# Down projection of a gated block as seven products of halves, with bias, compression and merge reordered

## The chip, the cores and the metric

The kernel runs on one core of one Trainium2 chip, as one launch. The metric is device time in microseconds (us), the median over runs. Engines are named as the profile names them: PE (TensorE matmul), DVE (VectorE), ACT (ScalarE), POOL (GpSimd), SP (SyncE, which here only issues DMAs). All tensors are fp32; every large product is made of three passes over tensors that were split into a high and a low part.

## What is computed

One layer of a hybrid decoder trunk over S=1024 tokens with D=1024 columns and F=2816 hidden columns:

```python
h = rmsnorm(x, norm_mix_g)
u, q, kc, vc, ks, vs, kw, vw, g_nsa, g_br = split(h @ w_in)
y_a = s5_mixer(u, ...) @ w_up_ssm            # state space, GELU, GLU
kc, vc = compress(kc, ...), compress(vc, ...) # gelu(blocks @ w1) @ w2
y_b = nsa_mixer(q, kc, vc, ks, vs, kw, vw, gates, rel_bias) @ w_up_nsa
x = x + (sigmoid(g_a) * y_a + sigmoid(g_b) * y_b) @ w_out
h = rmsnorm(x, norm_ffn_g)
x = x + (silu(h @ w_ffn_gate) * (h @ w_ffn_up)) @ w_ffn_down
out = rmsnorm(x, norm_final_g)
```

`rel_bias` is a table of 32 buckets by 8 heads; the attention adds its rows to the scores.

## The kernel before

**Splitting.** Each fp32 operand becomes a high part (ACT or POOL casts it to fp32r) and a low part (DVE subtracts the high part from the operand), in `Kernel.split` (lines 410 to 418). Each product is then three matmuls: high by high, high by low, low by high. Weights come in by DMA into tiles `wr` and are split into `wh` and `wl`. `Weights.next` (helper class at line 70) keeps two weight tiles split and four loaded ahead. The hidden values of the feed-forward come as `sr`, split into `shi` and `slo`.

**Order.** The order of every engine is the order in which the program issues its instructions. SP issues nearly all DMAs, and so takes them one after the other in that order; a DMA that waits holds back those behind it. The stages, in order of time, are these.

- Head: first norm, then `h @ w_in` as 448 groups of three matmuls of 512 columns (lines 406 to 408). The function `along(side, rate)` gives these groups out as cover: each `yield` of a side stage lets `rate` groups pass. The side stages are `s5_params` (line 666), `s5` (line 838), `compress` (line 971) and `glu` (line 1057). `s5_params` holds the bias step at lines 707 to 717: for each of 8 heads one plain fp32 matmul of 384 columns that spreads the bucket table over distances, a copy out of the matmul's bank, and a store to memory. `compress` loads eight weight blocks `w1` into three buffers. `glu` splits the values z of one token half, makes its products, and then does the other half.
- Up projection a (`up_a`), cut into parts of which 12 run ahead of the attention and the others in its first units; attention in 64 units; up projection b.
- Merge (line 1450): `@ w_out` for token tiles in the order of `units(...)`, the addition to x, the second norm (`norm`, `root`, `turned`), and the sums of input quarters that the next stage needs. `turn` runs these sums (T1 to T4, B22). `Winograd.first` (line 260) makes the first unit of the next stage with the last norms in between.
- Gate and up: class `Winograd` (line 123). The 44 blocks of 128 columns of both matrices go as 22 units. A unit forms two blocks (256 columns) for all tokens by seven products of half tokens, half depth and half of the two blocks in place of eight. It is 84 matmuls of 512 columns. POOL, DVE and ACT form sums of weight quarters and of products, and the finished hidden block is stored as two halves of 512 tokens each, `sd[f][0]` and `sd[f][1]`.
- Down (`down`, line 1598): two token halves, 22 blocks f of 128 hidden columns, four token tiles, two column halves, three passes: 1056 matmuls of 512 columns. Each f of a token half is 24 matmuls, one `sr` (256 KB) and one `wr` (512 KB). The first half's results are added to x and normed beside the second half; the second half's are added, normed, scaled and stored behind the last matmul, on DVE, ACT and for two scalings on POOL.

Of the kernel before, what the change touches and what calls it, by code (L numbers as in the profile page):

```python
# [16 lines left out]
P = 128  # L17
# [18 lines left out]
NPOW = 9  # L36

# [85 lines left out]
class Winograd:  # L123
# [136 lines left out]
    def first(self, norms, turn):  # L260
# [6 lines left out]
        self.product(1, 1, x1)  # L267
        next(norms)
        self.t2(0)
# [54 lines left out]
    def rest(self, n, early):  # L324
# [20 lines left out]
        self.t1(n + 1)  # L345
        if last:
            next(self.after)
# [7 lines left out]
        self.out(n, 1, 1, p5)  # L355
        self.product(n, 3, z, first=False)
# [9 lines left out]
        self.out(n, 1, 0, u3)  # L366

    def run(self, after):

        self.after = after  # L370
        for n in range(1, len(self.mats)):
            self.t3(n)
            self.sums(n + 1)
            if n > 1:
                self.p1(n)
            self.rest(n, n == 1)


class Kernel:
# [212 lines left out]
    def in_proj(self, specs, ev):  # L592

        nc = self.nc
        for c0, kind, dst in specs:
            w = self.W.next("w_in", 0, KD, c0, P)
            for h in range(2):
# [5 lines left out]
                elif kind in "qk":  # L603
# [5 lines left out]
                    nc.sync.dma_start(dst[0][:, tok], a.bitcast(F32))  # L609
                    nc.sync.dma_start(dst[1][:, tok], b.bitcast(F32))  # L610
                else:
# [5 lines left out]
                    nc.sync.dma_start(dst[:, tok], a)  # L617
# [20 lines left out]
    def s5_loads(self):  # L638
# [22 lines left out]
        self.rb = x("rb", 32, 8)  # L661
        dma(self.rb, A["rel_bias"])
        self.oh = x("oh", 32, 384)
        dma(self.oh, A["consts"][0:32, 874:1258])

    def s5_params(self):
# [39 lines left out]

        rbb = x("rbb", 32, 8, P)
        V.tensor_copy(rbb, self.rb[:, :, None].to_broadcast([32, 8, P]))
        yield
        for h in range(8):  # L710
            b = self.bank("c")
            nc.tensor.matmul(b[:, 0:384], rbb[:, h, :], self.oh, start=True, stop=True)
            s = tmp.tile([P, 384], F32, name="brs", tag="brs", bufs=2)
            (AC.copy if h % 2 else V.tensor_copy)(s, b[:, 0:384])
            nc.sync.dma_start(self.bd[h], s)
            yield
# [79 lines left out]
        yield  # L796

# [9 lines left out]
        V.tensor_tensor(self.Bq, self.Bq, w, op=OP.subtract)  # L807

# [29 lines left out]
    def s5(self):  # L838
# [63 lines left out]
        yield  # L902
        zb = None
# [67 lines left out]
    def compress(self, pool):  # L971
# [20 lines left out]
        def w1(j):  # L992
            w = pool.tile([P, 4, 256], F32, name="w1", tag="w1", bufs=3)
# [4 lines left out]
        ws = [w1(j) for j in range(3)]  # L998
# [18 lines left out]
        for which in range(2):  # L1017
            t = self.bank("c")
            for j in range(4):
# [6 lines left out]
                if 4 * which + j < 5:  # L1026
                    ws.append(w1(4 * which + j + 3))
# [29 lines left out]
    def glu(self, pool):  # L1057
        nc, V = self.nc, self.nc.vector
        for h in range(2):
            t = slice(512 * h, 512 * h + 512)  # L1060
            z = self.z[h]
            zs = [pool.tile([P, 4, 512], FR, name=n, tag=n) for n in ("zh", "zl")]
            for k in range(4):
                self.split(zs[0][:, k, :], zs[1][:, k, :], z[:, k, :], "act", "dve")
                yield
            yield
            yield
# [126 lines left out]
    def attention(self, pools, loads, up):  # L1194
# [163 lines left out]
        def start(n):  # L1358
            if n == 2:
# [16 lines left out]
            if n == 1:  # L1376
# [73 lines left out]
    def merge(self, pool, m, td, xd, ffn):  # L1450
# [90 lines left out]
        def units(tts, q, between):  # L1541

            banks = [self.bank("a") for _ in tts]
            for u in range(4):
# [13 lines left out]
                for f, *a in between.get(u, ()):  # L1558
                    f(*a)

        T = lambda tt, *what: [(turn, w, tt) for w in what]
        units((0, 1, 4, 5), 0, {(0, "m"): [(load, tt) for tt in (0, 1, 4, 5)] + [(ffn.factors,)],
# [3 lines left out]
                          1: [(turned, 0)] + T(4, "transpose", "sums"), 2: T(4, "T1", "B22")})  # L1566
# [11 lines left out]
    def down_loads(self, pool, sd):  # L1578
# [298 lines left out]
```

## Time and profile before

| | |
|---|---|
| runs | 1617.88, 1622.04, 1624.08 us (median 1622.04) |
| profiled execution | 1624.46 us, span 1622.7 us |
| PE busy | 1561.6 us (96% of the span) |
| DVE busy | 926.8 us (57%) |
| ACT busy | 634.6 us (39%) |
| POOL busy | 637.6 us (39%) |
| mean granted clock of PE | 0.979 |

The span is the time from the first to the last instruction of the profiled execution. A wait in the view of waits is idle time of one engine and the instruction that ended it: "PE c L1023 <- DMA w<-in_cmp_w_k" is a matmul of line 1023 into bank c that waited for a DMA which fills the tile w. A window row gives the busy time of each engine in a stretch, the number of its instructions in parentheses, the granted clock (PEclk), and what the DMA engines did. The end of a matmul is modelled, so the pace of matmuls is read from their starts.

### The profile page before, as it was taken

The numbers are of one execution on the slowest core, as the hardware profiler recorded it, in microseconds if no ns is written. First come the engines' busy times: TensorE is split into PE (matmuls) and PEld (weight loads), VectorE is DVE, ScalarE is ACT, GpSimd is POOL, SyncE is SP. The second block draws the span as 40 slices with busy tenths as digits, with TensorE's granted clock in tenths as the row PEclk, the third lists the DMA queues.
The fourth block names the chain that finished last, engine by engine and source line by source line (L and its number), as shares of the span: only waits on it lengthen the run. The fifth ranks groups of instructions, "written<-read, shape, count | busy, mean of one in ns | idle before, by whom it ended". The sixth has DMA issues, their size and how long they took to land. (4 is left out here: it accounts for less than half of the span.)

```text
span 1622.7 us, 22419 instructions
## 1 busy us (share of the span) xinstructions
PE 1561.6 (96%) x7928; PEld 1310.4 (81%) x7928; DVE 926.8 (57%) x1744; ACT 634.6 (39%) x1277; POOL 637.6 (39%) x740
## 2 busy tenths in 40 slices
PE   8998999998999999999999899999999999999995
PEld 8876888886877899998787777888888888888884
DVE  7346886632245899998857564444444445335433
ACT  5212334421220698898116543332333333233322
POOL 1005777610021455555450038677776661000001
PEclk9999999999999999999999989999999999999998
DMA  6342443339337712100666512223222214454551
GB/s 220 107 146 86 123 130 96 94 87 252 98 112 240 203 30 68 42 27 16 217 197 199 176 46 80 89 79 95 81 79 90 79 52 171 150 205 150 177 198 53
DMA packets 165607, 196.38 MB, mean 121 GB/s; under 512 B 20730, under 2 KB 119446, under 8 KB 165495
## 3 DMA queue, kind: packets, MB, share of 16 engines
q1 hardware_dynamic: 165495, 194.94, 38.7%
q8 instruction: 63, 1.03, 0.3%
q14 instruction: 49, 0.40, 0.1%
HBM read 144.96 MB, written 47.84 MB: 119 GB/s over the span
## 5 line engine op out<-in xcount | busy, mean ns | idle before, releaser
L418 DVE TENSOR_TENSOR wl<-wr,wh 128x1024 fp32r<-128x1024 f32 (+1 forms) x170 | 196.8, 1168 | 144.8 <-ACT wh L415 109.6
L406 PE MATMUL a<-hhi,wh 128*128 128x512 f32 x448 | 182.9, 408 | 0.0
L408 PE MATMUL a<-hhi,wl 128*128 128x512 f32 x448 | 178.0, 397 | 0.0
L407 PE MATMUL a<-hlo,wh 128*128 128x512 f32 x448 | 177.8, 397 | 0.0
L415 ACT CAST wh<-wr 128x1024 fp32r<-128x1024 f32 (+1 forms) x138 | 114.4, 844 | 157.2 <-PE a L220 41.6
L1285 POOL TENSOR_SCALAR P<-P,sum,gates 128x640 f32<-128x640 f32 (+3 forms) x192 | 124.8, 663 | 116.6 <-DVE sum L1279 73.5
L219 PE MATMUL a<-mhi,wh 128*128 128x512 f32 (+1 forms) x360 | 139.1, 386 | 2.2 <-ACT wh L415 1.8
L221 PE MATMUL a<-mhi,wl 128*128 128x512 f32 (+1 forms) x360 | 138.7, 385 | 0.8 <-DVE wl L418 0.8
L220 PE MATMUL a<-mlo,wh 128*128 128x512 f32 (+1 forms) x360 | 138.6, 385 | 0.0
L413 POOL TENSOR_SCALAR wh<-wr 128x1024 fp32r<-128x1024 f32 x32 | 34.0, 1064 | 226.8 <-PE a L407 168.8
L160 POOL TENSOR_SCALAR wr<-wr,gcol 128x256 f32<-128x256 f32 x176 | 92.7, 546 | 72.2 <-DVE mlo L474 67.9
L1314 DVE TENSOR_TENSOR PTl<-T,PTh 128x512 fp32r<-128x512 f32 (+3 forms) x200 | 104.2, 544 | 9.7 <-ACT PTh L1313 7.8
L406 PEld LDWEIGHTS a<-hhi,wh 128*128 128x128 f32 x448 | 85.0, 190 | 24.1 <-issue 6.2
L1265 ACT ACTIVATE P<-P,m 128x640 f32<-128x640 f32 (+7 forms) x128 | 95.7, 747 | 17.5 <-DVE m L1249 17.5
L408 PEld LDWEIGHTS a<-hhi,wl 128*128 128x128 f32 x448 | 85.0, 190 | 20.1
L418 DVE TENSOR_TENSOR slo<-sr,shi 128x512 fp32r<-128x512 f32 x44 | 32.0, 728 | 120.0 <-ACT shi L415 120.0
L407 PEld LDWEIGHTS a<-hlo,wh 128*128 128x128 f32 x448 | 85.1, 190 | 17.7
L1313 ACT CAST PTh<-T 128x512 fp32r<-128x512 f32 (+3 forms) x200 | 88.4, 475 | 20.7 <-PE T L1312 19.3
L1249 DVE CUSTOM_DVE_ANT_0 P<-S,B 128x640 f32<-128x640 f32 (+7 forms) x128 | 89.5, 700 | 5.0 <-PE S L1214 2.1
L418 DVE TENSOR_TENSOR wl<-S,wh 128x1024 fp32r<-128x1024 f32 x44 | 65.5, 1489 | 44.4 <-ACT wh L415 41.2
L1312 PE MATMUL T<-cst,P 128*128 128x128 f32 x592 | 87.2, 274 | 3.4 <-DVE PTl L1314 2.8
L415 ACT CAST shi<-sr 128x512 fp32r<-128x512 f32 x44 | 27.1, 619 | 154.4 <-PE c L1638 153.9
(427 smaller groups left out, 3992.1 us busy)
## 6 DMA issues: line engine op xcount, KB each, us to landing
wr<-in_w_ffn_down SPq DMA_DIRECT2D x44, 512.0 KB, 3.4
wr<-in_w_in SPq DMA_DIRECT2D x28, 512.0 KB, 4.1
wr<-in_w_out SPq DMA_DIRECT2D x24, 512.0 KB, 4.3
wr<-in_w_ffn_gate SPq DMA_DIRECT2D x22, 512.0 KB, 3.9
wr<-in_w_ffn_up SPq DMA_DIRECT2D x22, 512.0 KB, 3.7
sr<-sd SPq DMA_DIRECT2D x44, 256.0 KB, 4.0
gd<-evf SPq DMA_DIRECT2D x32, 256.0 KB, 2.6
Q<-qd SPq DMA_DIRECT2D x64, 128.0 KB, 3.0
```

The source lines that it names most:

```text
L160: self.K.nc.gpsimd.tensor_scalar(t[:, k], t[:, k], self.g[:, 4 * kh + k:4 * kh + k + 1], 1.0, op0=OP.mult, op1=OP.mult)
L219: mm(o, wh[:, k], bh[:, k, c], start=first and k == 0, stop=False, skip_group_check=True)
L220: mm(o, wh[:, k], bl[:, k, c], start=False, stop=False, skip_group_check=True)
L221: mm(o, wl[:, k], bh[:, k, c], start=False, stop=k == 3, skip_group_check=True)
L406: mm(ps, a, c, start=start and k == 0, stop=False, skip_group_check=True)
L407: mm(ps, a, d, start=False, stop=False, skip_group_check=True)
L408: mm(ps, b, c, start=False, stop=stop and k == nk - 1, skip_group_check=True)
L415: nc.scalar.copy(hi, src)
L418: (nc.gpsimd if lo_eng == "pool" else nc.vector).tensor_tensor(lo, src, hi, op=OP.subtract)
L1265: AC.activation(p[:, 0:nk], p[:, 0:nk], AF.Exp, bias=m[:, 0:1], scale=-1.0, accum_out=sm(0))
L1285: sc = lambda x, y, z: GP.tensor_scalar(x, x, a[:, y:y + 1], gate(z), op0=OP.mult, op1=OP.mult)
L1314: V.tensor_tensor(ol, t[:, 0:len(cc), :], oh, op=OP.subtract)
```

## The change

The text of the change has six parts.

1. `down` is one class of products as in gate and up: seven products over half of the tokens, half of the hidden depth (11 blocks) and half of the columns, in the order 1, 5, 6, 3, 7, 2, 4. That is 7 x 11 x 4 x 3 = 924 matmuls of 512 columns in place of 1056. Operands of the products are hidden halves `sd` themselves, or sums of them `ss`, and weight quarters or differences of them, which DVE makes (`combine`) in tiles `b0` to `b2` and `near` that stay loaded. Results are added to x on DVE as each product ends (`beside`).
2. The sums `ss` are made by `chain(f)`: four loads of 256 KB into one tile `ch` (one buffer), four additions and subtractions of 128x512 on DVE, four stores. Nine of the eleven chains run beside the last nine units of gate and up (`next(self.chain, None)` at four places of a unit), the last two beside the first eight blocks of product 1.
3. The end: token tiles 4 to 7 have their right column half done after product 2, so behind the last matmul each tile has one column half to add, square and norm. The last three blocks of product 4 are made tile by tile. POOL has no part in it. The norm and scaling of token tiles 0 to 3 stand beside blocks 3 to 7 of product 4.
4. Bias: the 8 heads go from `s5_params` to the start of `s5` (`bias`), with high and low parts of the table (two fp32r matmuls of 384 columns per head in place of one fp32 matmul). Stores of this step and of the input projection's results go out from ACT's queue.
5. Compression and GLU: four buffers for `w1`, four blocks loaded ahead, and in the first half one more `yield` per block; the second half of z is split before the first half's products.
6. Attention and merge: 10 in place of 12 parts of `up_a` before the attention, three more in its first units. In the merge, the table for the square root is loaded ahead (`one`), `turned(0)` and the sums of tile 5 stand later, and in `first` the sums `t2(0)` and tile 7's transposes and sums stand earlier.

```diff
@@ Winograd.first
+        self.t2(0)
         next(norms)
-        self.t2(0)
...
+        turn("transpose", 7, "ac")
         self.product(0, 2, x0, first=False)
-        turn("transpose", 7, "ac")
+        turn("sums", 7)
         turn("T1", 6)
         self.t3(0)
-        turn("sums", 7)
         self.product(1, 2, x1, first=False)
+        turn("T1", 7)
         self.p2out(0)
-        turn("T1", 7)
@@ Winograd.run
+            f = n - 2
+            self.chain = chain(f) if f >= NF // 2 else iter(())
+            next(self.chain, None)
             self.t3(n)
@@ input projection
-                    nc.sync.dma_start(dst[0][:, tok], a.bitcast(F32))
+                    nc.scalar.dma_start(dst[0][:, tok], a.bitcast(F32))
...
-                    nc.sync.dma_start(dst[:, tok], a)
+                    nc.scalar.dma_start(dst[:, tok], a)
@@ bias
-        for h in range(8):
-            b = self.bank("c")
-            nc.tensor.matmul(b[:, 0:384], rbb[:, h, :], self.oh, start=True, stop=True)
...
+            for i in range(2):
+                nc.tensor.matmul(b[:, 0:384], self.rbb[i][:, h, :], self.ohr, start=i == 0, stop=i == 1)
+            s = pool.tile([P, 384], F32, name="brs", tag="brs", bufs=2)
+            nc.scalar.copy(s, b[:, 0:384])
+            nc.scalar.dma_start(self.bd[h], s)
+            yield
@@ compress
-        ws = [w1(j) for j in range(3)]
+        ws = [w1(j) for j in range(4)]
...
-                if 4 * which + j < 5:
-                    ws.append(w1(4 * which + j + 3))
+                if which == 0:
+                    ws.append(w1(j + 4))
+                    yield
@@ merge
+        one = pool.tile([P, 1], F32, name="one")
+        V.memset(one, 1.0)
+        AC.activation(one, one, AF.Sqrt)
...
-                          1: [(turned, 0)] + T(4, "transpose", "sums"), 2: T(4, "T1", "B22")})
+                          2: [(turned, 0)] + T(4, "transpose", "sums"), (3, "m"): T(4, "T1", "B22")})
...
-                                (2, "m"): [(load, 6), (load, 7)] + T(5, "T1", "B22"), 2: T(5, "T3", "T2"),
-                                (3, "m"): T(5, "T4")})
-        units((2, 3), 1, {})
+                                (2, "m"): [(load, 6), (load, 7)] + T(5, "T1", "B22"), 2: T(5, "T3")})
+        units((2, 3), 1, {0: T(5, "T2"), 1: T(5, "T4")})
@@ chain and down
+    def chain(self, pool, sd, ss, f):
+        nc, V = self.nc, self.nc.vector
+        t, g = pool.tile([P, 4, 512], F32, name="ch", tag="ch", bufs=1), f - NF // 2
+        for i, src in enumerate((sd[g][0], sd[g][1], sd[f][0], sd[f][1])):
+            nc.sync.dma_start(t[:, i], src)
+        yield
+        a, b, c, d = (t[:, i] for i in range(4))
+        V.tensor_tensor(d, b, d, op=OP.add)
+        V.tensor_tensor(b, a, b, op=OP.subtract)
+        yield
+        V.tensor_tensor(a, d, a, op=OP.subtract)
+        V.tensor_tensor(c, c, a, op=OP.subtract)
+        yield
+        for i, n in enumerate((2, 3, 4, 1)):
+            nc.sync.dma_start(ss[g][n], t[:, i])
+        yield
...
+        order = [(p, f) for p in (1, 5, 6, 3, 7, 2, 4) for f in range(NH)]
...
+                if p in (5, 6, 7, 4):
+                    V.tensor_tensor(o, {5: s1, 6: s2, 7: s2, 4: s2}[p], o, op=OP.subtract)
...
+            mm(o, ah[:, t], bh, start=first, stop=False, skip_group_check=True)
+            mm(o, ah[:, t], bl, start=False, stop=False, skip_group_check=True)
+            mm(o, al[:, t], bh, start=False, stop=end, skip_group_check=True)
...
+            if p == 4 and f < 4:
+                V.tensor_tensor(half(4 + f, 1), half(4 + f, 1), gf[:, 512:D], op=OP.mult)
+            if p == 1 and f < 8:
+                if f % 4 == 0:
+                    sums["chain"] = self.chain(pool, sd, ss, NF - 2 + f // 4)
+                next(sums["chain"])
...
+            tt = f - 4
+            if 0 <= tt < 4 and p == 4:
+                scaled(tt, slice(0, D), self.rstd(dn, sums[tt]), "dve")
...
+        for n, (p, f) in enumerate(order[:last]):
+            split(n + 2)
+            load(n + 4)
+            combine(n + 3)
...
+            for tt in range(4):
+                products(n, tt)
+            beside(p, f)
+        split(len(order))
+        for tt in range(4):
+            for n in range(last, len(order)):
+                products(n, tt)
...
+            add(4 + tt, 0, U[tt])
+            square(half(4 + tt, 0), sums[4 + tt][:, 0:1])
+            if tt:
+                finish(tt - 1)
+        finish(3)
```

How the change moves instructions is shown at three places. First, SP's queue where down starts: `sd` is a store of hidden values (the last block's second store is the one from `u`), `sr` and `wr` are loads for down. Before:

```order
L244 DMA sd_8684<-p_12603 128x512
L244 DMA sd_8685<-u_12686 128x512
L1586 DMA sr<-sd_8651 128x512
L83 DMA wr<-in_w_ffn_down 128x1024
L1586 DMA sr<-sd_8653 128x512
```

And now, with the stores of the ninth chain (`ss` from `ch`) and the loads of the tenth (`ch` from `sd`):

```order
L245 DMA sd_8702<-p_12777 128x512
L245 DMA sd_8703<-u_12862 128x512
L1619 DMA ss_8738<-ch 128x512
L1619 DMA ss_8739<-ch 128x512
L1619 DMA ss_8740<-ch 128x512
L1619 DMA ss_8737<-ch 128x512
L1609 DMA ch<-sd_8679 128x512
L1609 DMA ch<-sd_8680 128x512
L1609 DMA ch<-sd_8701 128x512
L1609 DMA ch<-sd_8702 128x512
L1658 DMA sr<-sd_8673 128x512
L1651 DMA b_13007<-in_w_ffn_down 128x512
```

Eight DMAs of 256 KB stand between the last store of the hidden values and the next load that down's matmuls need.

Second, DVE at the same place (`slo` and `wl` are the low parts of one block's two operands, `u` the last sum of gate and up). Before:

```order
L365 TENSOR_TENSOR u_12686<-u_12686,c 128x512
L418 TENSOR_TENSOR slo<-sr,shi 128x512
L418 TENSOR_TENSOR wl<-wr,wh 128x1024
L418 TENSOR_TENSOR slo<-sr,shi 128x512
L418 TENSOR_TENSOR wl<-wr,wh 128x1024
```

And now:

```order
L368 TENSOR_TENSOR u_12862<-u_12862,c 128x512
L426 TENSOR_TENSOR slo<-sr,shi 128x512
L426 TENSOR_TENSOR wl<-wr,wh 128x512
L1612 TENSOR_TENSOR ch<-ch 128x512
L1613 TENSOR_TENSOR ch<-ch 128x512
L426 TENSOR_TENSOR slo<-sr,shi 128x512
L426 TENSOR_TENSOR wl<-wr,wh 128x512
L1615 TENSOR_TENSOR ch<-ch 128x512
L1616 TENSOR_TENSOR ch<-ch 128x512
```

The first pair of the tenth chain stands ahead of the split of down's fourth block (the splits of the first two stand farther up, beside gate and up), the second pair ahead of the fifth's.

Third, DVE late in product 4, the last product, for blocks 4 and 5 (`b` from two `b` is a weight difference, `x1f` the layer's x, `rstd` the factor of the norm). Before, the last blocks of down stood there, with nothing between:

```order
L418 TENSOR_TENSOR slo<-sr,shi 128x512
L418 TENSOR_TENSOR wl<-wr,wh 128x1024
L418 TENSOR_TENSOR slo<-sr,shi 128x512
L418 TENSOR_TENSOR wl<-wr,wh 128x1024
```

And now:

```order
L426 TENSOR_TENSOR slo<-sr,shi 128x512
L426 TENSOR_TENSOR wl<-near,wh 128x512
L1668 TENSOR_TENSOR b_13007<-b_14378,b_13007 128x512
L1707 TENSOR_TENSOR x1f<-x1f,c 128x512
L441 TENSOR_SCALAR rstd<-ssf_14672 128x1
L442 RECIPROCAL rstd<-rstd 128x1
L444 SCALAR_TENSOR_TENSOR rstd<-rstd 128x1
L448 SCALAR_TENSOR_TENSOR rstd<-rstd 128x1
L466 SCALAR_TENSOR_TENSOR x1f<-x1f,rstd,gfin 128x1024
L426 TENSOR_TENSOR slo<-sr,shi 128x512
L426 TENSOR_TENSOR wl<-b_13007,wh 128x512
```

A weight difference, an addition to x, and the norm and scaling of a finished token tile stand between the splits of two blocks.

## Rows read from the trace of the kernel before

**Rows 1.** The page, span.
```profile
span 1622.7 us, 22419 instructions
```

**Rows 2.** Waits of PE: line waited for, then us in total, times, longest us.
```profile
PE c L1023 <- DMA w<-in_cmp_w_k: 7.5, 2, 7.3
...
PE c L219 <- ACT T2h L415: 3.1, 1, 3.1
...
PE b L469 <- ACT xn L1488: 2.9, 1, 2.9
...
PE a L406 <- ACT zh L415: 2.7, 1, 2.7
...
PE a L1468 <- DVE x L1474: 2.2, 1, 2.2
```

**Rows 3.** Windows: stretches with waits, then stretches with a low clock behind waits.
```profile
140.00:160.00 20.00, 14.52 (x69) 10.71 (x68) 10.43 (x12) 4.62 (x8) 15.54 (x13) 1.00 0.26 81
...
520.00:549.00 29.00, 25.00 (x131) 20.64 (x130) 18.76 (x52) 10.84 (x32) 5.69 (x12) 1.00 0.67 208
...
925.00:932.00 7.00, 4.41 (x22) 3.44 (x21) 4.12 (x10) 5.58 (x10) 0.00 (x0) 0.95 0.60 203
...
398.58:402.21 3.63, 3.63 (x17) 3.63 (x18) 0.00 (x0) 0.00 (x0) 0.00 (x0) 0.50 1.07 273
455.50:460.30 4.80, 4.51 (x12) 3.37 (x13) 3.64 (x6) 1.94 (x4) 0.00 (x0) 0.64 0.71 269
860.10:866.50 6.40, 6.26 (x23) 5.34 (x24) 4.14 (x10) 4.81 (x8) 0.00 (x0) 0.51 0.42 110
...
955.90:962.00 6.10, 5.93 (x19) 5.06 (x20) 5.46 (x7) 2.02 (x3) 3.80 (x2) 0.50 0.17 38
```

**Rows 4.** Timeline of PE in the head: a bias matmul between two others.
```profile
97.77 0.91 PE L712 MATMUL c<-oh,rbb 32*128 32x384 f32 x2
...
98.95 0.39 PE L407 MATMUL a<-hlo,wh 128*128 128x512 f32 x1
```

**Rows 5.** Timeline of PE in down: start, duration; the same step 24 matmuls apart.
```profile
1499.57 0.39 PE L1637 MATMUL a<-wh,shi 128*128 128x512 f32 x1
...
1505.17 0.39 PE L1637 MATMUL a<-wh,shi 128*128 128x512 f32 x1
```

**Rows 6.** Timeline behind the last matmul: PE, then DVE, then POOL.
```profile
1604.33 0.40 PE L1639 MATMUL c<-wh,slo 128*128 128x512 f32 x1
...
1613.62 0.68 DVE L1616 TENSOR_TENSOR x1f<-x1f,c 128x512 f32<-128x512 f32 x1
1615.29 0.15 DVE L1647 TENSOR_REDUCE ssf<-ssf 128x1 f32<-128x2 f32 x1 [0.99 <-ACT scr L1606]
...
1616.46 0.75 DVE L458 SCALAR_TENSOR_TENSOR x1f<-x1f,rstd,gfin 128x512 f32<-128x512 f32 x1
...
1617.85 1.26 POOL L461 TENSOR_TENSOR x1f<-x1f,gfin 128x512 f32<-128x512 f32 x1
```

**Rows 7.** Timeline where down starts: DVE, then POOL.
```profile
1360.54 1.78 DVE L418 TENSOR_TENSOR slo<-sr,shi 128x512 fp32r<-128x512 f32 x1
1362.24 0.68 DVE L365 TENSOR_TENSOR u<-u,c 128x512 f32<-128x512 f32 x1
...
1366.16 0.68 DVE L418 TENSOR_TENSOR slo<-sr,shi 128x512 fp32r<-128x512 f32 x1
...
1363.42 1.75 POOL L243 TENSOR_TENSOR u<-u,u 128x512 f32<-128x512 f32 x1
```

**Rows 8.** DMA issues: from 1345 to 1375 us, then the whole page.
```profile
sd<-p SPq DMA_DIRECT2D x2, 256.0 KB, 2.1
...
sr<-sd SPq DMA_DIRECT2D x44, 256.0 KB, 4.0
```

**Rows 9.** Windows: 40 us of gate and up, then 40 us of down.
```profile
1200.00:1240.00 40.00, 40.00 (x178) 33.14 (x177) 18.09 (x20) 11.92 (x18) 27.30 (x30) 1.00 0.26 83
...
1400.00:1440.00 40.00, 40.00 (x173) 32.19 (x172) 13.60 (x15) 11.03 (x14) 0.00 (x0) 1.00 0.41 139
```

More of the change, by code (lines that the diff above doesn't have):

```diff
@@ L36 @@
 NPOW = 9
+NEAR = 6
 def run(gen, n=None):
@@ L355, in rest @@
         self.out(n, 1, 1, p5)
+        next(self.chain, None)
         self.product(n, 3, z, first=False)
@@ L902, in s5 @@
         yield
+        yield from self.bias(self.bs)
         zb = None
@@ L1589, in split @@
         def split(n):
             load(n)
+            combine(n)
             while len(parts) < min(n, len(order)):
-                hi, lo = (pool.tile([P, 512], FR, name=x, tag=x, bufs=3) for x in ("shi", "slo"))
-                self.split(hi, lo, raw[len(parts)], "act", "dve")
-                parts.append((hi, lo))
-        return order, parts, load, split
-    def down(self, pool, loads, xd):
-        nc, V, AC, mm = self.nc, self.nc.vector, self.nc.scalar, self.nc.tensor.matmul
-        order, parts, load, split = loads
-        x1 = {}
+                a = [pool.tile([P, 512], FR, name=x, tag=x, bufs=3) for x in ("shi", "slo")]
+                b = [self.W.hl.tile([P, 2, 512], FR, name=x, tag=x)[:, 0] for x in ("wh", "wl")]
+                self.split(*a, ra[len(parts)], "act", "dve")
+                self.split(*b, rb[len(parts)], "act", "dve")
+                parts.append((a, b))
@@ L1604, in square @@
+        yield
+        load(4)
+        yield
+        split(1)
+        yield
+        load(5)
+        yield
+        split(2)
+        load(NEAR)
+        yield
+        dn = self.pool("dn")
+        half = lambda tt, c: x1[tt][:, 512 * c:512 * c + 512]
+        U = [self.bank("a") for _ in range(4)]
+        Vs = [self.bank("bbcc"[i]) for i in range(4)]
+        sums = {}
         def square(x, ss):
-            scr = pool.tile([P, D], F32, name="scr", tag="scr", bufs=1)
+            scr = dn.tile([P, D], F32, name="scr", tag="scr", bufs=1)
@@ new lines, in x1_loads, with products @@
+        def x1_loads(tts, c):
+            for tt in tts:
+                if tt not in x1:
+                    x1[tt] = dn.tile([P, D], F32, name="x1f", tag="x1f", bufs=8)
+                nc.sync.dma_start(half(tt, c), xd[tt][:, 512 * c:512 * c + 512])
+        def products(n, tt):
+            p, f = order[n]
+            (ah, al), (bh, bl) = parts[n]
+            o, t = (U if p in (1, 6, 7, 4) else Vs)[tt], slice(P * tt, P * tt + P)
+            first, end = f == 0 and p in (1, 5, 2, 4), f == NH - 1
+            mm(o, ah[:, t], bh, start=first, stop=False, skip_group_check=True)
+            mm(o, ah[:, t], bl, start=False, stop=False, skip_group_check=True)
+            mm(o, al[:, t], bh, start=False, stop=end, skip_group_check=True)
@@ new lines, in finish @@
+        def finish(tt):
+            one = dn.tile([P, 1], F32, name="ssf1", tag="ssf1", bufs=8)
+            V.tensor_reduce(one, sums[4 + tt], axis=mybir.AxisListType.X, op=OP.add)
+            r = self.rstd(dn, one)
+            AC.activation(half(4 + tt, 1), half(4 + tt, 1), AF.Copy, scale=r)
+            nc.scalar.dma_start(self.out[P * (4 + tt):P * (5 + tt), 512:D], half(4 + tt, 1))
+            scaled(4 + tt, slice(0, 512), r, "dve")
+        last = len(order) - 3
+        for n, (p, f) in enumerate(order[:last]):
```

188 lines of the change are left out of this document (99 added, 89 removed).

## Prediction

> **What bounds the kernel now.** I read the page first: PE is busy nearly all of the span [rows 1], so what counts is PE's own work and the waits in front of it. The view of PE's waits names those waits: a 7.5 us wait for a compression weight, a few of 2 to 3 us in GLU and merge [rows 2]. Some waits are spread over several short rows, and for those I take windows: PE is idle 5.5 us of 140 to 160 (bias), 4.0 us of 520 to 549 (start of the attention) and 2.6 us of 925 to 932 [rows 3]. Behind four of the waits the windows show a granted clock near 0.5, which is 1.2 in place of 2.4 GHz; a stretch of length T at granted clock c loses T(1-c). Then the timelines: the same step of two successive blocks in down starts 5.60 us apart, 24 matmuls, so 0.2333 us each [rows 5]. Last, behind the last matmul (1604.33) stand 18.4 us to the span's end, of which 3.6 us lie behind the last computation (1617.85 + 1.26 = 1619.11) [rows 1, 6]. Gate and up show no idle PE in 40 us, with DVE busy 18.1 and POOL 27.3 [rows 9].
>
> **The change part by part**, against the profiled execution, 1624.5 us, 2.4 us above the median of the runs.
>
> *Bias.* The fp32 matmul and the one behind it take 1.18 us (97.77 to 98.95) [rows 4]; less 0.23 for the second, a head costs 0.95. Two fp32r matmuls of 384 columns are 2 x 0.75 x 0.2333 = 0.35. Eight heads give 4.8. The 5.5 us of idle [rows 3] stand where `s5` starts and PE has caught up with DVE and POOL; the eight heads now put 8 times 9 or 12 projection matmuls there, some 78 x 0.2333 = 18 us of cover, so I take 5.0 (0 to 5.5). The copies, all on ACT now, and 8 stores in ACT's queue lie beside ACT's 4.6 us in those 20. Sum 9.8. The other stores that leave SP for ACT cost ACT only its issue, in a stretch where ACT is mostly idle: nothing, up to 1 us if one of them holds back a cast.
>
> *Compression.* The wait of 7.5 us is for a fourth block whose load stood behind others in SP's order [rows 2]; four are now loaded ahead, and 18 in place of 9 projection matmuls (2.1 us more) stand between two blocks. The half clock behind it, 3.63 x 0.5 = 1.8 [rows 3], goes too. Of 9.3 I take 8.5, since four blocks in flight at once may hold up the first (4 to 9.3). The extra cover is not missed later: 81 projection matmuls are left behind GLU's end.
>
> *GLU.* z is split ahead: wait 2.7 [rows 2] and 4.8 x 0.36 = 1.7 of clock [rows 3], 4.4 (2 to 4.4).
>
> *Attention's start.* Two more pieces of matmuls cover 4.0 us of idle [rows 3]; I take 3 (0 to 4).
>
> *Merge.* First wait 2.9 and its clock 6.4 x 0.49 = 3.1: the square root's table is loaded ahead and the step stands one unit later, so 6.0. The wait of 2.2 for x also goes (one unit more of cover). The last two, 2.6, and 3.1 with 6.1 x 0.5 = 3.05 of clock [rows 2, 3], hang on DVE's chain of sums, which the change reorders but doesn't shorten: half of 8.75, 4.4. Sum 12.6 (6 to 17).
>
> *Down's matmuls.* 1056 - 924 = 132, at 0.2333: 30.8. Were the pace that of gate and up, 40/178 = 0.2247 with a few records missing [rows 9], it would be 29.7. The Trainium skill (TensorE: Matmul & The Clock Gate, Back-to-back issue gap) gives 215.7 ns for 512 columns at full clock, by which this term would be 28.5; the row has 0.2333, so the trace is slower than the page, and I keep the row.
>
> *The tail.* Behind the last matmul a tile now has one addition to x with its square (1613.62 to 1615.29, 1.67), the norm's factor (to 1616.46, 1.17), and one half scaled on DVE (0.75), then 3.6 to the end, and 0.4 for the matmul: 7.6 [rows 6]. The tile before it is finished on DVE between the square and the factor: about 1 us that the square doesn't cover. DVE needs 0.69 + 1.17 + 0.75 = 2.6 per tile where PE takes 9 x 0.2333 = 2.1: 2 us late after four. Some 10.4 for 18.4: gain 8 (5 to 10).
>
> *A new wait where down starts.* In SP's order the ninth chain's four stores and the tenth's four loads stand behind the last store of hidden values. `ch` has one buffer, so these loads wait until the stores have landed. Call the end of the last gate product D0. DVE's last sum and POOL's last multiplication (1.75) [rows 7] end at about D0+4; stores land 2.1 later; four more issues and a landing: D0+8.5; four loads land 4.0 after issue [rows 8]: about D0+12.5. DVE's pair on them stands ahead of the split of down's fourth block, and needs 2 x 0.68, and the split as much again: D0+15. PE wants this block after three others, 3 x 12 x 0.2333 = D0+8.4. Wait 6.6; the eleventh chain repeats it with some 1.5, and a half clock as behind the compression wait costs 1.8. I take 10. Lower bound 0 (all land in time), upper 14 (each step as slow as the slowest row).
>
> *A new wait in product 4.* DVE's splits and weight difference are 3 x 0.68 = 2.04 us a block [rows 7], an addition 0.68, the norm's factor without its reduction about 1.0, and a scaling of 1024 columns some 1.3 (0.75 for 512) [rows 6]: 5.0 in blocks 4 and 5, 4.3 in 6 and 7, against PE's 12 x 0.2333 = 2.8: 7.4 late after the four. The last three blocks' splits are wanted almost at once, 1.5 more, and one block (2.8) is split ahead: 6.1, I take 6 (2 to 10). In products 5 to 7 it is 2.04 + 0.68 = 2.7 where there is an addition: hidden, by 0.1 only.
>
> *Chains beside gate and up.* Nine units, four loads, four stores and four DVE operations of 0.7 each. A unit is 84 x 0.2247 = 18.9 us, DVE is busy 18.1/40 of it, 8.5, and gets 2.8 more; DMA moves 83 GB/s [rows 9], plus 2 MB in 18.9, 111 GB/s more, less than the 273 of a window [rows 3]. Hidden; I take 2 for the nine (0 to 14).
>
> Sum: 9.8 + 8.5 + 4.4 + 3 + 12.6 = 38.3 early; 30.8 + 8 - 10 - 6 - 2 = 20.8 late; 59.1 in all: 1624.5 - 59.1 = **1565**.
>
> **Rivals.**
> - *Down without waits.* The chain's data come earlier than I count and DVE's lookahead suffices: the 16 us are not paid, 1549. For it: the first product itself needs no sum of a chain, only DVE's order ties it to one. Against it: SP's and DVE's orders are fixed, and DVE's sum in product 4 is above PE's.
> - *The early waits move instead of going.* PE arrives sooner at the next slow step, DVE's or a DMA's: the change doesn't do half of what it says, 38.3/2 = 19 lost, 1584. For it: the waits for DVE are chains of DVE work that stay. Against: compression and bias are waits for order, not for work.
> - *DVE and POOL hold each other up in gate and up.* A `slo` of 512 columns took 1.78 us beside POOL and 0.68 alone [rows 7]. Four such operations per unit, each 1.1 longer, make 8.5 + 7.1 = 15.6 of 18.9 on DVE; the additions that free PE's banks stand behind them, and one such delay, not covered, is 1.1 to 1.8 per unit: 9 x 1.5 = 13.5 in place of 2, 1577. The Trainium skill (SBUF — State Buffer, Who interferes with whom) says that a DVE instruction with two SBUF inputs and a GpSimd instruction that reads SBUF shut each other out; the 1.78 us agree. That speaks against putting the chain there.
> - *Slower.* The chain's cycle gets onto the path of each unit: its loads (4.0), its DVE part (2.8), its stores (2.1) [rows 8] stand in SP's order among the weight loads, and the next weights wait for all: 8.9 x 9 = 80 in place of 2, 1565 - 2 + 80 = 1643. It decides from 61/9 = 6.8 us per unit. Against: DMA's share is 0.26 there [rows 9], and a unit leaves 18.9 us for the cycle.
>
> **How the numbers follow.** Forecast 0.43, down without waits 0.18, early waits moving 0.22, DVE against POOL 0.13, slower 0.03; 0.01 for mixtures near no change. 0.5% is 8 us, about what can be told from no change here. All but the slower case and the mixtures lie under 1616.5: faster 0.96, same 0.01, slower 0.03. The range reaches from a little under the first rival to a little over the second: 1545 to 1588; it leaves out the slower case and mixtures of two bad ones.
>
> **What would show it.** Right: no compression or bias row among PE's waits; down's matmuls 924, still 5.6 us per 24; behind D0 a wait of 5 to 9 us of PE for a low part at DVE, with the chain's pair in front of it; PE waiting for low parts late in product 4; 9 to 12 us behind the last matmul. Wrong: gate and up's units longer than 19 us, SP's weight loads landing after PE wants them, or PE idle in products 5 to 7, where DVE's margin is 0.1 us a block.

## The result and the profile after

The changed kernel takes 1604.63 us, median of 4 runs (1603.12 to 1606.01); the kernel before took 1623.06 (4 runs). The ratio is 0.9888, with a 95% interval of 0.9871 to 0.9905: 18 us or 1.1% less, and clear of the scatter. The prediction said 59 us less and a range of 1545 to 1588; the sign was right, the time lies outside the range. The profiled execution took 1604.1 us, 20.4 us less of span than before.

The page of the changed kernel, which answers to [rows 1]:

```profile
span 1602.3 us, 22657 instructions
...
PE 1528.9 (95%) x7796; PEld 1279.4 (80%) x7796; DVE 1015.7 (63%) x1916; ACT 659.4 (41%) x1354; POOL 642.0 (40%) x736
```

PE's busy time fell by 32.7 us, and the span by 20.4 only: PE stands idle 12.3 us more than before. The view of PE's waits of the changed kernel (line waited for, what ended it: us in total, times, longest) answers to [rows 2]; line numbers differ (matmuls of the input projection are L414 to L416 now, of merge L1491 to L1493, of gate and up L220 to L222, of down L1720 to L1722):

```profile
PE a L1721 <- DVE wl L426: 13.9, 4, 9.8
PE c L824 <- ACT brs L826: 6.6, 1, 6.6
PE b L222 <- DVE wl L426: 3.5, 6, 0.8
PE a L1491 <- DVE x L1497: 3.4, 2, 3.2
PE c L220 <- ACT T2h L423: 3.1, 1, 3.1
...
PE a L1491 <- ACT wh L423: 2.1, 2, 1.2
PE c L1045 <- DMA w<-in_cmp_w_k: 2.1, 1, 2.1
PE b L220 <- ACT wh L423: 2.0, 3, 1.1
PE a L1492 <- DVE wl L426: 1.5, 2, 0.8
PE b L477 <- ACT xn L1511: 1.5, 1, 1.5
...
PE a L416 <- DVE wl L426: 1.5, 1, 1.5
```

The compression wait is down from 7.5 to 2.1. GLU's wait of 2.7 for z is gone, and a projection matmul beside it waits 1.5 for the low part of a weight (L416). The forecast wait of down's matmuls for DVE is there (13.9 in all, 9.8 at once). Not forecast are 6.6 us for a bias copy of ACT, and waits of gate and up's matmuls (L222, and L220 for `wh`). In the merge the wait for xn is 1.5 in place of 2.9, but that for x is 3.4 in place of 2.2, that for `T2h` is 3.1 as before, and waits for weight parts are new (L1491 for `wh`, L1492).

To tell where the time went, both traces are cut at the same eight places (starts of PE's matmuls in the timelines, and one addition on DVE). Where projection matmuls moved across a cut, they are put back at 0.2333 us each: before, 1092 of the 1344 stand ahead of the first compression product, now 1041.

| stretch | now against before, us | forecast |
|---|---|---|
| to the first compression product (371.11; 379.41) | -8.3 + 51 x 0.2333 = **+3.6** | -9.8 (bias) |
| to the last compression product (408.39; 417.59) | -0.9 - 36 x 0.2333 = -9.3 | -8.5 |
| to the last projection matmul (481.16; 490.18) | +0.2 - 15 x 0.2333 = -3.3 | -4.4 (GLU) |
| to the last attention output (758.94; 768.65) | -0.7 | -3 |
| to the end of the second unit of gate and up, on DVE (969.24; 978.56) | **+0.4** | -12.6 (merge) |
| to down's first matmul (1355.54; 1357.52) | **+7.3** | +2 (chains) |
| to down's last matmul (1591.07; 1604.33) | -11.3 | -30.8 + 10 + 6 = -14.8 |
| to the end of the span (1602.3; 1622.7) | -7.1 | -8 |

The sum is -20.4. Three stretches make 32 of the missing 39 us: bias 13.4, merge 13.0, chains beside gate and up 5.3. A stretch of one execution is good to 1 or 2 us: in eight executions of kernels with the changed merge (the changed kernel, `early`, and six of the runs below) the merge's stretch took 209.4 to 212.0 us.

### The profile page after: what moved, and what is told of

It is laid out like the page before. It is cut to its first block, busy times and chain, and to the rows that moved or that the text cites. A ratio compares the mean times of both kernels' runs of the same rounds, so it can differ in the third digit from the quotient of the medians.

```text
span 1602.3 us, 22657 instructions
## 1 busy us (share of the span) xinstructions
PE 1528.9 (95%) x7796; PEld 1279.4 (80%) x7796; DVE 1015.7 (63%) x1916; ACT 659.4 (41%) x1354; POOL 642.0 (40%) x736
## 4 chain that ended last, share of the span: by engine, by line
PE 70%; DVE 10%; DMA 6%; ACT 5%; POOL 4%; issue 3%; SPq 1%; ACTq 0%; DVEq 0%; POOLq 0%
PE a L414 8%; PE a L416 7%; PE a L415 7%; PE O L1353 4%; PE a L220 4%; PE a L221 4%; PE a L222 4%; PE T L1335 3%; PE S L1237 3%; DVE wl L426 2%; DMA wr<-in_w_out 2%; ACT wh L423 2%; PE a L1721 2%; PE a L1722 2%; PE b L221 2%
## 5 line engine op out<-in xcount | busy, mean ns | idle before, releaser
L426 DVE TENSOR_TENSOR wl<-wr,wh 128x512 fp32r<-128x512 f32 (+1 forms) x142 | 160.0, 1139 | 140.8 <-ACT wh L423 96.1
L414 PE MATMUL a<-hhi,wh 128*128 128x512 f32 x448 | 183.5, 410 | 0.0
L416 PE MATMUL a<-hhi,wl 128*128 128x512 f32 x448 | 178.8, 399 | 1.5 <-DVE wl L426 1.5
L220 PE MATMUL a<-mhi,wh 128*128 128x512 f32 (+1 forms) x360 | 139.1, 386 | 0.9 <-ACT p L235 0.3
L222 PE MATMUL a<-mhi,wl 128*128 128x512 f32 (+1 forms) x360 | 138.5, 385 | 1.0 <-DVE rstd L441 1.0
L423 ACT CAST wh<-wr 128x512 fp32r<-128x512 f32 (+1 forms) x110 | 78.0, 728 | 129.2 <-DMA wr<-in_w_out 40.9
L414 PEld LDWEIGHTS a<-hhi,wh 128*128 128x128 f32 x448 | 85.4, 191 | 22.1 <-issue 4.1
L416 PEld LDWEIGHTS a<-hhi,wl 128*128 128x128 f32 x448 | 85.4, 191 | 22.1 <-DVE wl L426 1.9
L423 ACT CAST shi<-sr 128x512 fp32r<-128x512 f32 x77 | 47.7, 620 | 122.5 <-issue 53.8
L426 DVE TENSOR_TENSOR slo<-sr,shi 128x512 fp32r<-128x512 f32 x77 | 54.5, 708 | 49.6 <-ACT shi L423 49.6
```

The lines of the kernel that those rows point to most:

```text
L220: mm(o, wh[:, k], bh[:, k, c], start=first and k == 0, stop=False, skip_group_check=True)
L222: mm(o, wl[:, k], bh[:, k, c], start=False, stop=k == 3, skip_group_check=True)
L414: mm(ps, a, c, start=start and k == 0, stop=False, skip_group_check=True)
L416: mm(ps, b, c, start=False, stop=stop and k == nk - 1, skip_group_check=True)
L423: nc.scalar.copy(hi, src)
L426: (nc.gpsimd if lo_eng == "pool" else nc.vector).tensor_tensor(lo, src, hi, op=OP.subtract)
```

## The experiments

Runs went to several chips, each beside the kernel before on the same chip, so the ratio to that kernel is what compares. The changed kernel stands at 0.9888.

**The change in two halves.** `early` has all parts ahead of gate and up, with the old down; `downonly` has the new down and its chains, with the old rest.

> Bias, compression, GLU, attention's start and merge as in the change; gate and up, and down as before. Theory 1 (the prediction on record): the early waits go, 38 us less than the kernel before, about 1586. Theory 2 (the waits moved): the marks of the changed trace stand 9 us earlier where gate and up begin, so about 1614, with a wait of 6 to 7 us for a bias copy of ACT in place of those for DVE, and new waits for w_out's casts in the merge.

Measured: 1616.40, ratio 0.9967 (0.9955 to 0.998), 5 us less than before. The wait of 6.7 us for ACT's bias copy is in its trace. Theory 1 falls: the early parts, which were forecast at 38 us, are worth 5 in these runs (9.3 by the stretches above).

> Down as seven products with its chains; everything ahead of gate and up as before. Theory 1 (the prediction): 21 us less than the kernel before, about 1603. Theory 2 (the chain's cycle at SP costs in gate and up as well): 18 less behind gate and up and 7 more in them, so 11 less, about 1612; four of the last units 2 to 4 us longer than the others.

Measured: 1612.27, ratio 0.9943 (0.9928 to 0.9957), 9 to 10 us less. The early parts being absent, it shows 9.9 us of one wait at the start of down and the waits in gate and up (L222 3.3, L220 1.5 from 1190 us on). Theory 2 has the time right; its cause is taken up below.

**Bias: whose order is at fault.** The wait stands between these rows of the changed kernel's timelines, ACT first, then DVE (start, duration, what, and in brackets idle time before and what ended it):

```profile
116.59 0.56 ACT L638 COPY uv<-a 128x64 f32<-128x64 f32 x4 [3.46 <-DVE uv L638]
118.92 0.56 ACT L638 COPY uv<-a 128x64 f32<-128x64 f32 x4 [1.78 <-DVE uv L638]
...
120.39 0.48 ACT L826 COPY brs<-c 128x384 f32<-128x384 f32 x1 [0.41 <-ACT evf L624]
```
```profile
114.47 1.52 DVE L896 TENSOR_TENSOR w<-m,m 128x512 f32<-128x512 f32 x1 [0.95 <-POOL m L895]
115.91 0.60 DVE L638 COPY uv<-a 128x64 f32<-128x64 f32 x4
116.43 1.88 DVE L426 TENSOR_TENSOR wl<-wr,wh 128x1024 fp32r<-128x1024 f32 x1
118.23 0.60 DVE L638 COPY uv<-a 128x64 f32<-128x64 f32 x4
```

The block u of the projection is copied out in eight pieces, four by DVE and then four by ACT into the same tile. DVE comes to its four only behind its state space operations; ACT sits idle for them, and the copies of the bias banks, which moved into ACT's queue behind these, can't free the two banks. PE's third bias head waits at 113.90 to 120.92.

```diff
-        for e, cp in enumerate((nc.vector.tensor_copy, nc.scalar.copy)):
+        for e, cp in enumerate((nc.scalar.copy, nc.scalar.copy)):
```

> The changed kernel with all eight copies of a u block on ACT in place of four on DVE and four on ACT. Theory 2 (ACT stands behind DVE's copies when PE wants a bias bank back, but DVE and POOL set the end of that stage): the wait of 6.6 us for the bias copy goes, but PE then waits about as much longer for the first transposed way-in tile of the state space stage; 0 to 3 us less. Rival (only ACT's order is at fault): the wait and the low clock behind it go, 8 us less, about 1596.

Measured: 1593.94, ratio 0.9818 (0.9794 to 0.9842), some 11 us less than the changed kernel. ACT in that trace:

```profile
108.23 1.92 ACT L638 COPY uv<-a 128x64 f32<-128x64 f32 x16
109.89 0.76 ACT L624 COPY evf<-a 128x512 f32<-128x512 f32 x1
...
111.06 0.48 ACT L826 COPY brs<-c 128x384 f32<-128x384 f32 x1 [0.41 <-PE c L824]
```

The bias copy comes 9.3 us earlier, no wait for a bias bank is left, and the wait for the first way-in tile is 1.2 us (1.5 in the changed kernel) and not longer. The first compression product starts at 359.69, with as many projection matmuls ahead of it, where it was 371.11: 11.4 of the 13.4 us that the bias stretch lacked. So theory 2 falls and the rival holds: the cover that the prediction counted was enough, and ACT's order took the gain away. (The edit also takes the four copies, 0.6 us a time, off DVE; that ACT waited for them is what the rows above show.) From 121 to 127 us the granted clock in the changed kernel is 0.50, 1.2 GHz, behind the 6.6 us in which PE stood still; that was 3 us more:

```profile
121.00:127.00 6.00, 6.00 (x14) 4.21 (x14) 2.75 (x3) 1.55 (x3) 2.02 (x2) 0.50 0.59 201
```

**Merge: waits that change places.** `merge_undone` takes the merge and the first unit back to the old order.

> The changed kernel with the merge's order, and that of the first unit of gate and up, as before, and without the early square root. Theory 1 (the prediction: the merge's new order is worth 12.6 us): 1617. Theory 2 (its waits only changed places: a wait for the early square root's place on ACT, for x and for weight splits in place of those for xn and wh): 1602 to 1607, no difference that can be told.

Measured: 1604.33, ratio 0.9881 (0.9861 to 0.9901): no gain of the new order is left to see, and the 12.6 us are ruled out. The stretch from the last attention output to the second unit's end took 211.4 us with the old order in this run, 208.4 in `downonly` and 209.9 in the kernel before; with the new order it took 209.4 to 212.0. Its rows before and then now (length, busy time of PE, PEld, DVE, ACT, POOL, then granted clock):

```profile
768.65:978.60 209.95, 196.90 (x888) 161.86 (x888) 143.97 (x209) 84.39 (x121) 62.52 (x57) 0.93 0.51 164
```
```profile
758.94:969.20 210.26, 191.95 (x887) 156.01 (x887) 143.54 (x209) 83.97 (x122) 61.57 (x57) 0.98 0.51 164
```

The matmuls are the same. PE is busy 5.0 us less, at a clock of 0.98 in place of 0.93, and idle 18.3 us in place of 13.1. So much of the low clock went, as forecast, and waits for DVE and ACT, all but two of them under 1.6 us, took the whole gain. DVE is as busy as before. `merge_undone` has most of both with the old order (PE busy 193.7 us at a clock of 0.96, idle 17.7), so the new order is not what made them. One place where a moved step makes PE wait, on DVE in the changed kernel:

```profile
860.46 0.69 DVE L482 TENSOR_TENSOR mlo<-b,mhi 128x512 fp32r<-128x512 f32 x1
...
865.32 0.68 DVE L426 TENSOR_TENSOR mlo<-b,mhi 128x512 fp32r<-128x512 f32 x1
865.92 1.28 DVE L1497 TENSOR_TENSOR x<-x,a 128x512 f32<-128x512 f32 x2
```

The step that was put one unit later (`turned(0)` and tile 4's sums) now stands ahead of the addition that gives a bank back, eight operations with a weight split among them, and PE waits 3.2 us for that (L1491 <- x). Two more runs tried single waits. `sqrt_from_eps` drops DVE's memset from in front of the early square root:

```diff
-        V.memset(one, 1.0)
-        AC.activation(one, one, AF.Sqrt)
+        AC.activation(one, self.eps, AF.Sqrt)
```

> The changed kernel with the early square root of the merge taken from a constant that is there from the start, so that ACT doesn't wait for DVE's memset. Theory (that memset stands behind DVE's work, and the early square root holds back the cast of w_out's next block): PE's waits of 1.2 and 0.8 us at 814 and 815 us go, 2 us less, at the edge of what can be told; the trace decides. Rival (the cast was late by its DMA): the waits stay.

Measured: 1603.26, ratio 0.9889 (0.9866 to 0.9912), no difference. Between 805 and 860 us PE's wait for the cast fell from 2.1 to 0.8, and in its place that for x came to 1.6 (0.2 in the changed kernel): 3.9 us of waits in all, as in the changed kernel. Over the whole merge stretch PE waits 2.4 us less in this trace, but its clock is 0.96 in place of 0.98, and the stretch is as long (210.3 us). `combined_turn` moves the step behind the addition, on top of `combined` (below):

```diff
-                          2: [(turned, 0)] + T(4, "transpose", "sums"), (3, "m"): T(4, "T1", "B22")})
+                          3: [(turned, 0)] + T(4, "transpose", "sums", "T1", "B22")})
```

> The combined kernel with tile 0's turning and tile 4's sums in the merge placed behind the additions to x of tiles 1 and 5, not ahead of them. Theory (in the merge PE waits for DVE's order: some eight operations of that step stand ahead of the addition that gives a bank back): the 3.0 us wait for x goes, and the sum of waits between 840 and 980 falls by 2 to 4 us: about 1575. Rival (DVE has more work there than PE has cover, so that the wait moves to the next step that hangs on the same operations, the sums of tile 4 or the last T2): no gain, 1577 to 1580.

Measured: 1579.94, ratio 0.9734 (0.9707 to 0.9762), against 0.9729 of `combined`. Waits of PE from 790 to 990 us, `combined` and then `combined_turn`:

```profile
PE a L1494 <- DVE x L1500: 4.0, 2, 3.0
...
PE b L480 <- ACT xn L1514: 1.5, 1, 1.5
...
PE b L1536 <- ACT xn L1514: 0.3, 1, 0.3
```
```profile
PE b L1536 <- ACT xn L1514: 2.4, 2, 2.1
PE b L480 <- ACT xn L1514: 1.9, 2, 1.4
PE a L1494 <- DVE x L1500: 1.6, 1, 1.6
```

The 3.0 us for x went, and waits for xn of 0.5 and 2.1 came in the step that was moved. In all three runs the time stays where it was.

**Chains beside gate and up.** In the changed kernel, SP, DVE, POOL and ACT in one of the longer units:

```profile
1200.27 0.32 SPq L245 DMA_DIRECT2D sd<-u  x1
1200.68 1.97 SPq L1619 DMA_DIRECT2D ss<-ch  x4
1205.07 1.74 SPq L1609 DMA_DIRECT2D ch<-sd  x4
```
```profile
1208.13 2.42 DVE L426 TENSOR_TENSOR wl<-wr,wh 128x512 fp32r<-128x512 f32 x2 [0.97 <-ACT wh L423]
1211.66 0.69 DVE L1612 TENSOR_TENSOR ch<-ch 128x512 f32<-128x512 f32 x1 [1.10 <-DMA wr<-in_w_ffn_gate]
...
1213.00 0.68 DVE L353 TENSOR_TENSOR u<-p,b 128x512 f32<-128x512 f32 x1
```
```profile
1213.81 1.62 POOL L354 TENSOR_TENSOR p<-u,p 128x512 f32<-128x512 f32 x1 [3.80 <-issue]
```
```profile
1215.46 0.63 ACT L241 ACTIVATE p<-p 128x512 f32<-128x512 f32 x1 [6.84 <-POOL p L354]
...
1217.14 1.03 ACT L423 CAST wh<-S 128x1024 fp32r<-128x1024 f32 x1
```

The chain's loads leave at 1205.07, 2.4 us after SP was done with the stores ahead of them, which free the one buffer. DVE's first pair on them (its wait of 1.1 is put down to the weight load behind them; it reads `ch` alone) comes at 1211.66 and takes 1.3 us, ahead of the sum u; POOL's p waits for u, ACT's SiLU for p, and the cast of the next weight sum stands behind the SiLU. PE waits there for `wh` and `wl` in every second unit, the ones with a SiLU (the last sums of successive units start 17.4 and 21.6 to 23.5 us apart in turn, where 18.4 and 19.6 was the rule). Two edits tell whether it is the wait for the loads or the DVE work itself. `stores_first`:

```diff
-        self.out(n, 1, 0, u3)
         next(self.chain, None)
+        self.out(n, 1, 0, u3)
```

> The changed kernel with one line moved: a chain's four stores are issued ahead of the last hidden store of the unit, not behind it, so they no longer wait for POOL. Theory 2 (chain loads wait for the landing of stores that stand behind POOL's last product): chain loads land about 4 us earlier, gate and up lose their 7 us of waits, the wait at the start of down falls from 9.8 to about 5.5: 11 to 12 us less than the changed kernel, about 1593. Rival (DVE and POOL hold each other up, the chain's four DVE operations are what costs): gate and up as in the changed kernel, at most 4 us less, about 1600.

Measured: 1596.81, ratio 0.9845 (0.9827 to 0.9863), 7 us less than the changed kernel and between the two forecasts. DVE waits in front of none of the nine chains' pairs any more (in all 3.4 us in the changed kernel). Gate and up are 3 us shorter in the trace (914.28 to 1351.89, where it was 914.75 to 1355.54), PE's waits beside the chains under 0.3 us each; but from the second unit's end they still take 382.6 us, where it was 386.3 and 379.0 before the change. So the wait for the loads is about half of the price. The wait at the start of down only fell to 8.8: SP's four stores now left at 1355.45 and the loads at 1361.22, still behind them. `late_pairs` moves DVE's pairs one step later in each unit:

```diff
         self.t1(n + 1)
-        next(self.chain, None)
...
         V.tensor_tensor(u3, u3, c, op=OP.add)
+        next(self.chain, None)
         self.out(n, 1, 0, u3)
```

> The changed kernel with the chain's two DVE pairs one step later in each unit of gate and up (behind the third sum and behind the last one). Theory 2 (DVE waits for chain loads ahead of a sum that POOL and ACT need): units of 19.0 us throughout, 7 us less, about 1597, start of down as in the changed kernel. Rival (DVE and POOL hold each other up): the same number of DVE operations stands beside POOL, so no gain, about 1604.

Measured: 1602.21, ratio 0.9886 (0.987 to 0.9901), which can't be told from the changed kernel. Its trace shows where the two cancel: gate and up take 434.3 us from their first matmul to down's first (912.74 to 1347.01), 6.5 less, with no wait of PE from 1190 to 1347; but down, whose first splits stand behind the pairs, takes 2.7 more to its last matmul. From the second unit's end gate and up take 379.6 us, 0.6 more than before the change, with DVE as busy there as in the changed kernel (207.2 and 208.6 us) and POOL too (268.0 and 265.5), and with 2.7 us of waits for loads in front of the pairs. So neither the DVE work itself nor its overlap with POOL costs the time: the pair's place ahead of u does, with its own 1.3 us and its wait. Theory 2 had the place right, and its wait for loads is half of the price. The runs' medians don't show the 3.8 us that are left over in the trace.

**The start of down.** DVE and SP in the changed kernel, which answer to [rows 7, 8]:

```profile
1360.76 1.78 DVE L426 TENSOR_TENSOR wl<-wr,wh 128x512 fp32r<-128x512 f32 x1
1372.73 0.69 DVE L1612 TENSOR_TENSOR ch<-ch 128x512 f32<-128x512 f32 x1 [10.19 <-DMA ch<-sd]
...
1374.07 0.68 DVE L426 TENSOR_TENSOR slo<-sr,shi 128x512 fp32r<-128x512 f32 x1
```
```profile
1362.02 0.32 SPq L245 DMA_DIRECT2D sd<-u  x1
1362.39 2.01 SPq L1619 DMA_DIRECT2D ss<-ch  x4
1366.83 1.75 SPq L1609 DMA_DIRECT2D ch<-sd  x4
1368.62 0.43 SPq L1658 DMA_DIRECT2D sr<-sd  x1
```

DVE stands idle for 10.2 us in front of the chain's pair, as the prediction described. `chains_later` puts the pairs where their loads have landed:

```diff
-            if p == 1 and f < 8:
-                if f % 4 == 0:
-                    sums["chain"] = self.chain(pool, sd, ss, NF - 2 + f // 4)
+            k = f + {1: 0, 5: NH}.get(p, 99)
+            if k in (3, 10):
+                sums["chain"] = self.chain(pool, sd, ss, NF - 2 + (k == 10))
+            if k in (3, 6, 7, 8, 10, 13, 14, 15):
                 next(sums["chain"])
```

> The changed kernel with the last two chains spread over later blocks: the tenth chain's loads beside block 3 of product 1, its DVE pairs beside blocks 6 and 7, its stores beside block 8; the eleventh's loads beside block 10, its pairs beside blocks 2 and 3 of product 5, its stores beside block 4. Theory 2 (DVE stands in front of the chain's loads, and the split that PE needs is behind it): the waits of 9.8 and 1.4 us and the half clock behind them go, 11 to 13 us less than the changed kernel, about 1592. Rival (down's own loads of hidden values and weights land late there, whatever DVE does): a wait of 5 us or more stays, at most 5 us less, about 1600.

Measured: 1595.76, ratio 0.9826 (0.9804 to 0.9848), 10 us less than the changed kernel. PE's waits from 1340 us to the end:

```profile
PE a L1721 <- DVE wl L426: 3.6, 3, 2.5
PE b L1721 <- DVE wl L426: 1.4, 2, 0.7
```

The wait of 9.8 is gone (of the first row's waits 0.5 stands at down's start, and the rest late in product 4), and 1.4 came where the pairs now stand, in product 5. From down's first to its last matmul it is 224.7 us, 10.8 less. The rival falls: down's own loads were there.

**Product 4.** `p4_pool` gives the scaling of tiles 0 to 3 to POOL:

```diff
-                scaled(tt, slice(0, D), self.rstd(dn, sums[tt]), "dve")
+                scaled(tt, slice(0, D), self.rstd(dn, sums[tt]), "pool")
```

> The changed kernel with the scaling of token tiles 0 to 3 beside product 4 on POOL in place of DVE. Theory 1 (DVE has more to do in blocks 4 to 7 of product 4 than PE takes for them): the waits of 3.7 us in the last three blocks go, and the half clock behind them, 4 us less, about 1600. Rival (the last blocks' casts and splits are wanted all at once by the order of the tail): the waits stay, no gain.

Measured: 1613.16, ratio 0.9937 (0.9918 to 0.9957), 8 us more than the changed kernel; in the trace 6.0 of them lie between down's first and last matmul. Neither theory had that. DVE, then POOL, in this run:

```profile
1575.26 1.54 DVE L1668 TENSOR_TENSOR b<-b,b 128x512 f32<-128x512 f32 x1
...
1576.96 2.09 DVE L444 SCALAR_TENSOR_TENSOR rstd<-rstd 128x1 f32<-128x1 f32 x1
```
```profile
1574.27 1.98 POOL L468 TENSOR_SCALAR x1f<-x1f,rstd 128x1024 f32<-128x1024 f32 x1 [0.39 <-DVE rstd L448]
1576.34 2.70 POOL L469 TENSOR_TENSOR x1f<-x1f,gfin 128x1024 f32<-128x1024 f32 x1
```

An operation on one element per partition took 2.09 us, where it takes 0.22 elsewhere, and ended as POOL's ended (1579.05 and 1579.04); the weight difference took 1.54 in place of 0.69. `gf_early` takes work off DVE without POOL:

```diff
-            if p == 4 and f < 4:
-                V.tensor_tensor(half(4 + f, 1), half(4 + f, 1), gf[:, 512:D], op=OP.mult)
+            if p == 2 and f > 6:
+                V.tensor_tensor(half(f - 3, 1), half(f - 3, 1), gf[:, 512:D], op=OP.mult)
```

> The changed kernel with the four multiplications of finished right halves by the final norm's row beside blocks 7 to 10 of product 2 in place of blocks 0 to 3 of product 4. Theory 1 (DVE's own work is the bound in product 4): DVE is free 2.4 us earlier there, PE's waits of 3.7 us in the last three blocks fall to about 1.5 and the half clock behind them may go, 2 to 4 us less than the changed kernel, about 1601. Rival (the tail's order alone makes the waits): no change.

Measured: 1605.30, ratio 0.9901 (0.9882 to 0.9921): no change; PE's three waits in the last blocks are 0.65, 0.56 and 2.5 us, as in the changed kernel. In its timeline DVE now idles 0.3 to 0.9 us a block up to block 3 of product 4, each time until ACT's cast `shi` of the next block, and has one pause of 0.6 us, for ACT, from 1563.96 to the last split, where blocks 4 to 7 with their scalings come. So the time won ahead of them isn't kept. The rival, that the tail's order makes the waits, had the right outcome; that DVE's work of the four blocks is what counts was not tried by itself.

**Together.** `combined` takes the copies of `uv_act`, the chains of `chains_later`, the pairs of `late_pairs` in all units but the last, `gf_early` and `sqrt_from_eps`.

> The changed kernel with u's copies all on ACT, the last two chains later, the chain's DVE pairs later in all units but the last, the multiplications by the final norm's row in product 2, and the early square root from the constant. If the causes are independent, the gains of the single runs add: 10.5 (u's copies), 9 (last chains), 3 to 6 (pairs), 2 to 4 (multiplications), 2 (square root): 27 to 32 less than the changed kernel, about 1575. Rival (they hide one another, since a stage that comes earlier waits at the next): 1585 or more.

Measured: **1578.01** (1576.28 to 1579.08), ratio 0.9729 (0.9708 to 0.9749): 26 us less than the changed kernel, faster than both; 27 was the lower end. By the stretches, 10.0 of it lie ahead of the last attention output, 2.0 in the merge, 5.6 in gate and up and 8.1 in down: `late_pairs`' gain in gate and up is kept, which its loss in down had hidden. So the gains nearly add. What was worth nothing alone (the square root, the multiplications) is not shown to be worth anything here.

## Why the prediction was wrong, point by point

- *Down's matmuls*: right. 924 in place of 1056, 0.232 us apart (1449.92 to 1455.49 for 24 of them), forecast 0.2333.
- *The tail*: right, 11.2 us from the last matmul's start; forecast 10.4, though its own terms, 7.6 + 1 + 2, add up to 10.6.
- *The wait at the start of down*: right in mechanism and place, and `chains_later` shows its cause. In size 9.8 and 2.6 of clock (0.63 over 7 us behind it) stand against 6.6 and 1.8; the 1.5 for the eleventh chain came to 0.2.
- *Product 4*: forecast 6, found 3.7 of waits, and 1.7 of clock (0.89 over the 15 us from 1575). The size is right; that DVE's work makes it is not shown, since `gf_early` took four multiplications of 0.7 us away ahead of it and gained nothing.
- *Compression and GLU*: right, 9.3 and 3.3 for 8.5 and 4.4; neither was tried by itself.
- *Bias*: wrong by 13.4 us. The step that failed is "The copies, all on ACT now, and 8 stores in ACT's queue lie beside ACT's 4.6 us in those 20". ACT had the time and not the order: its queue held copies that waited for DVE, for 6.6 us of PE and 3 of clock, and `uv_act` gives back 11.4 of the 13.4. The prediction priced the busy time of the engine that took the work over, and did not ask what stands ahead in its queue.
- *Merge*: wrong by 13.0 us. The step that failed is to take the waits for xn and x for gone, and half of the last two, because their steps were moved. The low clock did go for the most part (0.93 to 0.98, 5.0 us of PE's busy time), and waits for DVE and ACT grew by 5.2; `merge_undone` has most of both with the old order, and in `sqrt_from_eps` and `combined_turn` a wait that was taken away came back as another wait or as a lower clock. What keeps the stretch at 208 to 212 us is open. The rival "the early waits move instead of going", at 0.22, was right for this stretch; for bias, the larger loss, it was not: a new wait came there from ACT's order, and `uv_act` takes it away.
- *Chains beside gate and up*: the term "Hidden; I take 2 for the nine (0 to 14)" was mis-sized: 7.3. DVE's and DMA's load left room, as counted; the price is the first pair's place in DVE's order, ahead of a sum that POOL and ACT need, and about half of it is the wait for loads behind stores. The rival on DVE and POOL had 13.5 for another cause; `late_pairs` speaks against it there, and `p4_pool` for it elsewhere.
- *Attention's start*: 0.7 for 3; why is open, it was not tried by itself.

## What to carry to other kernels

Work that moves to an idle engine has to be placed in that engine's order: look at what stands ahead of it there and whom that waits for, not at the engine's busy share. Where PE waits for a chain on another engine that nothing shortens, count a moved wait at zero until a run shows it gone; and put an operation that needs a load as late in its engine's order as its result allows.

## What the runs showed of the hardware

DVE was held up by POOL far beyond its own work: in `p4_pool` a DVE operation of 128x1 with its inputs in SBUF took 2.09 us (0.22 elsewhere) beside a POOL multiplication of 128x1024 that took 2.70. In the prediction such an overlap cost 1.1 us a time. The Trainium skill (SBUF — State Buffer, Who interferes with whom) says that a DVE instruction with two SBUF inputs and a GpSimd instruction that reads SBUF contend, that the lock is exclusive, and that the order of issue decides which of them is blocked; the ends at 1579.05 and 1579.04, with POOL's start ahead of DVE's (1576.34 and 1576.96), agree. By it, `p4_pool` should not have been expected to gain.
